# Plain float32 products in place of three split ones, in the query, expert-table and state-space input products of a two-layer backbone

## The chip, the cores and the metric

The kernel runs on one NeuronCore of a Trainium2 chip (trn2). The metric is device microseconds of one execution, the median of several runs. PE is TensorE (PEld its weight load), DVE is VectorE, ACT is ScalarE, POOL is GpSimd, SP is the engine whose queue issues most DMAs.

## The reference, cut to what matters

Two layers, each a token mixer and then a PEER channel mixer, over 512 latent tokens and (in the first layer) 256 context tokens of width 1024, all in float32. Layer 0 mixes with an mLSTM, layer 1 with a Mamba-2 state-space scan (SSD) whose inputs are one product with `w_in` and a five-tap convolution.

```python
def block(xb):                       # PEER, 128 tokens
    q = (xb @ wq).reshape(P_BLOCK, P_HEADS, 2, P_DK // 2)
    s = jnp.einsum('thcd,hcnd->thcn', q, sub_keys)
    s_top, i_top = lax.top_k(s, P_TOPK)          # 16 of 128, twice per head
    ...
    best_s, best_j = lax.top_k(cand_s, P_TOPK)   # 16 of the sums
    idx = jnp.take_along_axis(cand_i, best_j, axis=-1)
    gate = jax.nn.softmax(best_s, axis=-1)
    act = jax.nn.gelu(jnp.einsum('td,thkd->thk', xb, u[idx]))
    return jnp.einsum('thk,thkd->td', gate * act, v[idx])

def prep(h):                         # SSD input
    z, xbc, dt_raw = jnp.split(h @ w_in, [B_DI, B_DI + B_CONV_CH], axis=-1)
    xbc = jax.nn.silu(dw_conv(xbc, conv_w, conv_b))
```

`u` and `v` are tables of 16384 rows, 128 blocks of 128.

## The kernel before, in words

**Split products.** Most weight products are made as three products of the type `float32r`: a weight block `raw` (two slices of 128x512, 512 KB, three buffers) comes from memory, ACT casts it to `whi` (L173), DVE subtracts to get `wlo` (L175), the activations are split alike (`split`, L185 and L186), and `mm3` (L208 to L210) adds hi x hi, hi x lo and lo x hi in PSUM. `ch_steps` uses this with channels as output rows, `tok_steps` with tokens.

**PEER of the latent tokens** (`peer_lat`, one call per layer). `affine_in` transposes and scales the tokens into `pinh`/`pinl`. `peer_scores` makes the queries (4 blocks x 8 slices x 4 outputs x 3 products of 128x512), multiplies them with the keys (L782), and DVE takes the top 16 of each row of 128 (`top16`, L789 to L794). Then a loop over the first 66 blocks of the table `u` (NPRE = 66, `prefix`): 24 products of 128x384 (8 slices x 3), a GELU on ACT (`w`, L977), a store to `aD`. Woven into that loop are `gate_steps`, for 3 of the 4 token tiles (NDENSE = 3): `select` on DVE (L828 to L830 its costly part), then 16 rounds of a one-hot `oh` (L1016), `oa` (L1021), two `og` (L1027) on DVE, and 16 small products on PE per round (L1032), whose result goes to the dense gate table `gD`. The fourth tile, and in layer 0 the context tokens, go another way: `gather_steps` fetches single table rows by indirect DMA on POOL (L860) and DVE multiplies them (L867 for `u`, L878 for `v`). A gather is made to wait for a product (`paced`).

When the gates of all three tiles are written, `dense` runs over all 128 blocks of `v`: `w` is read back from `aD` (blocks below 66) or made by `scores` with `mm3` (the other 62), multiplied with the gates (L1057), split, and multiplied with `v` in 18 products of 128x512.

**The SSD layer.** `ssd_ctx` makes 6 input blocks of the context (256 columns), convolves them, and runs the states; `ssd_lat` makes 12 blocks of the latent tokens (512 columns) and weaves them with the scan (`scan`), in which DVE, ACT and PE take turns and each step reads `bcs` from memory.

**Order.** Each engine runs its instructions in one fixed order, which the scheduler sets from the program's order and its own idea of the times; `PER`, `R_PRE` and other rates say in the program how many gate or gather steps follow a block. SP's queue is in order too.

Of the kernel before, what the change touches and what calls it, by code (L numbers as in the profile page):

```python
# [65 lines left out]
def backbone(ctx: ExitStack, tc: tile.TileContext, A: dict, out: bass.AP):  # L66
# [162 lines left out]

    def ch_block(wt, n, kc, xh, xl, T, eng=None, bank=None):  # L230
# [72 lines left out]
    def make_in(pool, i, cond, js, jc, get, T, xh, xl):  # L303
        sh, sc = mrow(i, cond, js, pool), mrow(i, cond, jc, pool)
        for t in range(T // P):
            x = get(t, pool)
            y = big(pool)
            nc.vector.tensor_tensor(y, x, sc, OP.mult)
            nc.vector.tensor_tensor(y, y, sh, OP.add)
            for half in range(2):  # L310
                o = smb()
                for c in range(4):
                    nc.tensor.transpose(o[:, c * P:(c + 1) * P],
                                        y[:, (half * 4 + c) * P:(half * 4 + c + 1) * P], ident)
                s = (slice(None), slice(half * 4, half * 4 + 4), slice(t * P, (t + 1) * P))
                split(xh[s], xl[s], o.rearrange("p (c t) -> p c t", c=4))
# [43 lines left out]
    def affine_in(pool, i, cond, js, jc, z, T, xh, xl):  # L360


        sh = col(modD[i][cond, js * DM:(js + 1) * DM], pool, "a_sh")
        sc = col(modD[i][cond, jc * DM:(jc + 1) * DM], pool, "a_sc")
        g2, b2 = col(A["ln_g"][i, 0], pool, "a_g"), col(A["ln_b"][i, 0], pool, "a_b")
        nc.vector.tensor_tensor(g2, g2, sc, OP.mult)
        nc.vector.tensor_tensor(b2, b2, sc, OP.mult)
        nc.vector.tensor_tensor(b2, b2, sh, OP.add)
        g, b = row(A["ln_g"][i, 0], pool), row(A["ln_b"][i, 0], pool)
        def mapped(t, half):  # L370
            o = (mxb if half and AFB else smb)()
            to_tok(o, z(t)[:, half * 512:(half + 1) * 512], 4)
            x = pool.tile([P, 4, P], F32, tag="ax", name="ax", bufs=3)
            for c in range(4):
                k = half * 4 + c
                oc = o[:, c * P:(c + 1) * P]
                if c % 2:
                    nc.scalar.activation(x[:, c], oc, AF.Identity, scale=g2[:, k:k + 1], bias=b2[:, k:k + 1])
                else:
                    nc.vector.tensor_scalar(x[:, c], oc, g2[:, k:k + 1], b2[:, k:k + 1], op0=OP.mult, op1=OP.add)  # L380
            return x

        todo = [(t, half) for t in range(T // P) for half in range(2)]
        x = mapped(*todo[0])
        for (t, half), nxt in itertools.zip_longest(todo, todo[1:]):
            y, x = x, mapped(*nxt) if nxt else None
            s = (slice(None), slice(half * 4, half * 4 + 4), slice(t * P, (t + 1) * P))
            split(xh[s], xl[s], y)
# [373 lines left out]
    def peer_scores(pool, i, cond, T, h, inh, inl, side=None):  # L762
# [128 lines left out]
    def peer_lat(i, h, pp, then=lambda: None, close=lambda: None):  # L891
# [7 lines left out]
        with tc.tile_pool(name="pt", bufs=1, reuse_waits="tile") as xp:  # L899
            xh = xp.tile([P, 8, LAT], F32R, name="pinh")  # L900
            xl = xp.tile([P, 8, LAT], F32R, name="pinl")
# [7 lines left out]
            vt, it = peer_scores(xp, i, 0, LAT, h, xh, xl)  # L909
# [25 lines left out]
            with tc.tile_pool(name="pd", bufs=1, reuse_waits="tile") as dp:  # L935
                acc = dense(xp, dp, i, gD, aD, nd, xh, xl)
# [32 lines left out]
    def scores(xp, i, i2, xh, xl, TD, w):  # L969

        so = smb()[:, :TD]
        for half, (uh, ul) in enumerate(wpair(A[f"uT{i}"][i2].rearrange("h p c -> p h c"))):
            for k in range(4):
                s = slice(k * P, (k + 1) * P)
                kk = half * 4 + k
                mm3(so, uh[:, s], ul[:, s], xh[:, kk, :TD], xl[:, kk, :TD], kk == 0, kk == 7)
        nc.scalar.activation(w, so, AF.Gelu_apprx_tanh)  # L977

    def gate_steps(pp, bp, vt, it, gD, t, iot4):
# [117 lines left out]
    def dt_prep(pool, sp, inh, inl, nt):  # L1097
# [5 lines left out]
        with tc.tile_pool(name="sw", bufs=1, reuse_waits="tile") as wq:  # L1103
            w8 = wq.tile([P, 8, 64], F32, name="w8")
            nc.sync.dma_start(w8, A["s_dt"])
            w8h = wq.tile([P, 8, 64], F32R, name="w8h")
            w8l = wq.tile([P, 8, 64], F32R, name="w8l")
            split(w8h, w8l, w8)
            for k in range(8):
                mm3(o[:64, :nt * P], w8h[:, k], w8l[:, k], inh[:, k, :nt * P], inl[:, k, :nt * P], k == 0, k == 7)  # L1110
# [53 lines left out]
    def ssd_in(pool, h):  # L1164
# [3 lines left out]
        inh = pool.tile([P, 8, T], F32R, name="inh")  # L1168
        inl = pool.tile([P, 8, T], F32R, name="inl")

        def steps():
            with tc.tile_pool(name="slr", bufs=1, reuse_waits="tile") as q:
                make_in(q, 1, 0, 0, 1, lambda t, p_: h(t), T, inh, inl)
            dts = dt_prep(pool, pool, inh, inl, nt)
            dtr = next(dts)
            yield inh, inl, dtr, acD
# [10 lines left out]
    def ssd_ctx_in(pool, get, hcp, cinp):  # L1187
# [6 lines left out]
        inh = cinp.tile([P, 8, CTX], F32R, tag="cinh", name="cinh", bufs=1)  # L1194
        inl = hcp.tile([P, 8, CTX], F32R, tag="h_ctx", name="cinl", bufs=1)
        for t, y in enumerate(ys):
            for half in range(2):
# [3 lines left out]
                split(inh[s], inl[s], o.rearrange("p (c t) -> p c t", c=4))  # L1201
        return inh, inl

    def ssd_ctx(inh, inl, SD, lat, rest):
        T, nt = CTX, CTX // P
        with tc.tile_pool(name="sc", bufs=1, reuse_waits="tile") as pool:
            bt = pool.tile([P, nt, 1024], F32, name="bt")
            with tc.tile_pool(name="scv", bufs=1, reuse_waits="tile") as q:
                dts = dt_prep(pool, q, inh, inl, nt)
                for n_, n in enumerate((4, 5, 0, 1, 2, 3)):  # L1210
# [13 lines left out]
                    for c, o in enumerate(ch_block(A["s_in"], 4 + n, 8, inh, inl, T,  # L1224
# [19 lines left out]
    def ssd_lat(h, SD, inh, inl, dtr, acD, dts):  # L1244
# [4 lines left out]
        with ExitStack() as es_:  # L1249
            q = es_.enter_context(tc.tile_pool(name="slq", bufs=1, reuse_waits="tile"))  # L1250

            def channels(n, dst):
                for c, o in enumerate(ch_block(A["s_in"], 4 + n, 8, inh, inl, T)):
# [11 lines left out]
            def project_xz(n):  # L1265
                xt[n] = q.tile([P, nt, 512], F32, tag="xt", name="xt", bufs=2)
                zt[n] = q.tile([P, nt, 512], F32, tag="zt", name="zt", bufs=2)
                for c, o in enumerate(ch_block(A["s_in"], 4 + n, 8, inh, inl, T)):
# [7 lines left out]
                for t, o in enumerate(tok_block(A["s_in"], n, 8, inh, inl, T)):  # L1276
# [234 lines left out]
    cin, rest = peer_lat(0, hl, pp, lambda: ssd_ctx_in(pp, hc, hcpool, cinp), ppx.close)  # L1511
# [3 lines left out]
    with tc.tile_pool(name="sl", bufs=1, reuse_waits="tile") as lp:  # L1515
        lat = ssd_ctx(*cin, SD, ssd_in(lp, hl), rest)
# [79 lines left out]
```

## Time and profile before

| | |
|---|---|
| median of 3 runs | 5928.29 us (5920.93 to 5936.06) |
| profiled execution | 5929.8 us, span 5928.0 us, granted clock 0.937 |
| busy: PE, PEld, DVE | 5272.5 us (89%), 4330.6 us (73%), 4623.1 us (78%) |
| busy: ACT, POOL | 2508.2 us (42%), 1517.6 us (26%) |
| DMA | 1406.96 MB, 236 GB/s over the span |

Busy times are sums over instructions, and a PE matmul's time includes its way through the array, so that a new matmul starts long before the last has ended: what a product costs in a stream is the distance of two starts. The shares are means over stages with different limits; the stages are read one by one.

### The profile page before, as it was taken

The page shows a single profiled execution, that of the slowest core. Times are in us where ns is not written, and L with a number is a line of the kernel's source. Part 1 is how long each engine was busy: PE and PEld are TensorE (multiplying, and loading weights), DVE is VectorE, ACT ScalarE, POOL GpSimd, SP SyncE. Part 2 cuts the span into 40 slices and gives each one's busy share as a digit, 9 for nine tenths or more (in the row PEclk, how much of TensorE's full clock was granted, in tenths as well). Part 3 has the DMA queues.
Part 4 walks back from the last instruction along what each step waited for, and adds up shares of the span by engine and source line. Part 5 has one row for each costly group of instructions (what it writes and reads, how often), then busy time and mean ns, then how long its engine had stood idle before and what let it go on. Part 6 is the DMA issues. An engine that isn't in the chain of part 4 may idle for free.

```text
span 5928.0 us, 76907 instructions
## 1 busy us (share of the span) xinstructions
PE 5272.5 (89%) x25708; PEld 4330.6 (73%) x25708; DVE 4623.1 (78%) x8960; ACT 2508.2 (42%) x5186; POOL 1517.6 (26%) x1284
## 2 busy tenths in 40 slices
PE   6899999999997875998699999788877998799998
PEld 4688777766663444898578899667666898688997
DVE  6743567877676788999888889767776998788888
ACT  4643454322222333344333333477874344333333
POOL 1300001345544445121033444000001011133442
PEclk8999999999998887998799999899888998799999
DMA  6765555898879987566698999433334357798996
GB/s 211 240 191 156 161 164 163 282 333 303 301 248 320 327 313 254 168 198 213 207 340 315 347 336 332 155 97 96 104 110 125 121 180 250 254 339 321 345 339 234
DMA packets 655799, 1406.96 MB, mean 237 GB/s; under 512 B 62760, under 2 KB 237496, under 8 KB 650920
## 3 DMA queue, kind: packets, MB, share of 16 engines
q1 hardware_dynamic: 507944, 865.11, 44.1%
q0 software_dynamic: 147456, 536.94, 25.7%
q8 instruction: 201, 3.29, 0.2%
q14 instruction: 198, 1.62, 0.1%
HBM read 1278.10 MB, written 123.70 MB: 236 GB/s over the span
## 4 chain that ended last, share of the span: by engine, by line
PE 40%; DVE 13%; DMA 13%; issue 6%; ACT 4%; POOL 1%; DVEq 0%; SPq 0%; ACTq 0%; POOLq 0%
PE mm L208 6%; PE mm L209 6%; PE mm L210 6%; PE sm L210 4%; PE sm L208 4%; PE sm L209 4%; DMA g<-in_v_dram,idv 4%; DMA g<-in_u_dram,idx 3%; DVE wlo L175 2%; DMA bcs<-acD 2%; PE mx L1032 2%; PE mx L210 1%; PE mx L208 1%; PE mx L209 1%; DMA raw<-in_v_dram 1%
## 5 line engine op out<-in xcount | busy, mean ns | idle before, releaser
L173 ACT CAST whi<-raw 128x512 fp32r<-128x512 f32 x2032 | 1227.0, 619 | 1815.4 <-PE mm L209 575.7
L175 DVE TENSOR_TENSOR wlo<-raw,whi 128x512 fp32r<-128x512 f32 x1979 | 1348.3, 695 | 499.8 <-ACT whi L173 488.0
L860 POOL DMA_INDIRECT g<-in_u_dram,idx x512 | 623.4, 1218 | 1465.8 <-PE mx L210 418.0
L860 POOL DMA_INDIRECT g<-in_v_dram,idv x512 | 679.3, 1327 | 888.0 <-DVE acc L878 316.8
L878 DVE SCALAR_TENSOR_TENSOR acc<-g,act,acc 128x1024 f32<-128x1024 f32 x508 | 655.7, 1291 | 156.2 <-DMA g<-in_v_dram,idv 153.6
L867 DVE CUSTOM_DVE_ANT_0 g<-g,xb 128x1024 f32<-128x1024 f32 x512 | 622.4, 1220 | 161.8 <-DMA g<-in_u_dram,idx 160.6
L210 PE MATMUL sm<-pinh,wlo 128*128 128x384 f32 x2048 | 693.1, 342 | 14.8 <-DVE wlo L175 14.2
L208 PE MATMUL sm<-pinh,whi 128*128 128x384 f32 x2048 | 697.1, 340 | 4.3 <-ACT w L977 3.0
L209 PE MATMUL sm<-pinl,whi 128*128 128x384 f32 x2048 | 694.2, 339 | 0.0
L209 PE MATMUL mm<-wlo,wh 128*128 128x512 f32 x1024 | 400.6, 394 | 11.1 <-DVE wlo L175 11.0
L210 PEld LDWEIGHTS sm<-pinh,wlo 128*128 128x128 f32 x2048 | 386.0, 189 | 23.2 <-DVE wlo L175 22.5
L210 PE MATMUL mm<-whi,wl 128*128 128x512 f32 x1024 | 393.8, 391 | 3.2 <-DVE wl L186 3.2
L208 PEld LDWEIGHTS sm<-pinh,whi 128*128 128x128 f32 x2048 | 386.5, 189 | 12.6 <-ACT w L977 5.6
L208 PE MATMUL mm<-whi,wh 128*128 128x512 f32 x1024 | 362.5, 396 | 35.0 <-ACT wh L185 31.0
L209 PEld LDWEIGHTS sm<-pinl,whi 128*128 128x128 f32 x2048 | 386.6, 189 | 5.5
L209 PE MATMUL mm<-xcl,whi 128*128 128x256 f32 (+1 forms) x1024 | 349.2, 346 | 8.9 <-DVE xcl L186 8.9
L210 PE MATMUL mm<-xch,wlo 128*128 128x256 f32 (+1 forms) x1024 | 332.0, 349 | 21.6 <-DVE wlo L175 21.4
L208 PE MATMUL mm<-xch,whi 128*128 128x256 f32 (+1 forms) x1024 | 344.3, 349 | 5.1 <-ACT xch L185 4.0
L208 PE MATMUL mm<-inh,whi 128*128 128x512 f32 (+1 forms) x768 | 285.8, 376 | 11.1 <-ACT cva L401 6.9
L1057 DVE TENSOR_TENSOR w<-w,gtb 128x384 f32<-128x384 f32 x256 | 232.5, 912 | 63.8 <-DMA gtb<-gD 28.6
L209 PE MATMUL mm<-inl,whi 128*128 128x512 f32 (+1 forms) x768 | 279.9, 366 | 0.0
L1032 PE MATMUL mx<-og,oa 128*128 128x128 f16 x1536 | 199.2, 297 | 86.3 <-DVE og L1027 86.2
(478 smaller groups left out, 10947.3 us busy)
## 6 DMA issues: line engine op xcount, KB each, us to landing
raw<-in_uT_dram SPq DMA_DIRECT2D x256, 512.0 KB
raw<-in_v_dram SPq DMA_DIRECT2D x256, 512.0 KB
raw<-in_w_qk_dram SPq DMA_DIRECT2D x128, 512.0 KB
raw<-in_ada_w_dram SPq DMA_DIRECT2D x96, 512.0 KB
raw<-in_w_up_dram SPq DMA_DIRECT2D x96, 512.0 KB
gD<-sg SPq DMA_DIRECT2D x48, 1024.0 KB
gtb<-gD SPq DMA_DIRECT2D x32, 1536.0 KB
raw<-in_s_in_dram SPq DMA_DIRECT2D x72, 512.0 KB
```

What stands on the lines that cost most here:

```text
L173: nc.scalar.copy(hi, raw[:, u])
L175: (eng or next(los["eng"])).tensor_tensor(lo, raw[:, u], hi.bitcast(F32), OP.subtract)
L208: nc.tensor.matmul(o, sh, mh, start=start, stop=False)
L209: nc.tensor.matmul(o, sh, ml, start=False, stop=False)
L210: last["pe"] = nc.tensor.matmul(o, sl, mh, start=False, stop=stop)
L860: d = nc.gpsimd.indirect_dma_start(out=g_, out_offset=None, in_=tab, in_offset=bass.IndirectOffsetOnAxis(ap=ix[:, k:k + 1], axis=0))
L867: nc.vector.tensor_tensor_reduce(out=g_, in0=g_, in1=xb, scale=1.0, scalar=0.0, op0=OP.mult, op1=OP.add, accum_out=act[:, k:k + 1])
L878: nc.vector.scalar_tensor_tensor(acc, g_, act[:, k:k + 1], acc, OP.mult, OP.add)
L1032: nc.tensor.matmul(g4[:, k * P:(k + 1) * P], oa[:, f, :, k], og[:, u, :, k], start=u == 0, stop=u == 1)
L1057: nc.vector.tensor_tensor(w, w, gt[0][:, :, j], OP.mult)
```

## The change

Queries of the latent tokens, the 66 blocks of `u` ahead of the dense pass, and all products with the SSD input weights become one plain float32 product each, straight from `raw` (`wraws`), with unsplit activations (`px`, `inx`, `cinx`). The casts and subtractions of those weights and activations go. The dense pass still needs `pinh`/`pinl` for its last 62 blocks, so these are now split from `px` behind the gates. `oh` gets a second buffer. The queries of the context tokens, the mLSTM, both down products and the dense pass stay as they are.

```diff
+    def wraws(wt, n, kc):
+        for k in range(0, kc, 2):
+            raw = raw2(wt[n, k:k + 2].rearrange("k p c -> p k c"))
+            for u in range(2):
+                yield raw[:, u]
+                tick()
...
+    def ch_whole(o, wt, n, kc, x):
...
+        for k, w in enumerate(wraws(wt, n, kc)):
+            for c in range(4):
+                last["pe"] = nc.tensor.matmul(o[c], w[:, c * P:(c + 1) * P], x[:, k, :T], start=k == 0 and not pair,
...
     def ch_block(wt, n, kc, xh, xl, T, eng=None, bank=None):
-        for _ in ch_steps(o, wt, n, kc, xh, xl, eng):
+        for _ in ch_whole(o, wt, n, kc, xh) if xl is None else ch_steps(o, wt, n, kc, xh, xl, eng):
...
@@ affine_in, peer_scores
+            if xl is None:
+                x = xh[:, half * 4:half * 4 + 4, t * P:(t + 1) * P]
...
-                for _ in ch_steps(os_, A["wq"][i], n, 8, inh, inl):
+                for _ in ch_steps(os_, A["wq"][i], n, 8, inh, inl) if cond else ch_whole(os_, A["wq"][i], n, 8, inh):
...
@@ peer_lat
-                scores(xp, i, i2, xh, xl, TD, w)
+                so = smb()[:, :TD]
+                raw = raw2(A[f"uT{i}"][i2].rearrange("h p c -> p h c"))
+                for kk in range(8):
+                    last["pe"] = nc.tensor.matmul(so, raw[:, kk // 4, kk % 4 * P:(kk % 4 + 1) * P], x[:, kk, :TD],
+                                                  start=kk == 0, stop=kk == 7)
+                nc.scalar.activation(w, so, AF.Gelu_apprx_tanh)
...
+                for k in range(8):
+                    split(xh[:, k], xl[:, k], x[:, k, :TD])
...
@@ gate_steps
-                oh = bp.tile([P, 4, P, 4], BF16, tag="oh", name="oh", bufs=1)
+                oh = bp.tile([P, 4, P, 4], BF16, tag="oh", name="oh", bufs=2)
...
@@ ssd_ctx, ssd_lat
-                    for c, o in enumerate(ch_block(A["s_in"], 4 + n, 8, inh, inl, T,
+                    for c, o in enumerate(ch_block(A["s_in"], 4 + n, 8, x_in, None, T,
```

The scheduler also moves instructions. On DVE, at two gate rounds of layer 1's prefix loop, this stands before (`fi`, `g` belong to `select`):

```order
6643 L175 TENSOR_TENSOR wlo_42332<-raw_42312,whi_42330 128x512
6644 L1016 TENSOR_TENSOR oh_40553<-iot4_40246,ct_40406 128x2048
6645 L175 TENSOR_TENSOR wlo_42384<-raw_42380,whi_42382 128x512
6646 L830 TENSOR_REDUCE fi_41478<-g_41455 128x16
6647 L828 TENSOR_TENSOR g_41456<-placek_75,bjb_41477 128x800
6648 L1021 TENSOR_TENSOR oa_40555<-oh_40553,ct_40406 128x1024
6649 L1027 TENSOR_TENSOR og_40557<-oh_40553,cm_40415 128x1024
6650 L1027 TENSOR_TENSOR og_40569<-oh_40553,cm_40415 128x1024
6651 L175 TENSOR_TENSOR wlo_42400<-raw_42380,whi_42398 128x512
6652 L829 TENSOR_TENSOR g_41455<-g_41456 128x800
```

and this now, at a like place of the same loop on DVE:

```order
6299 L864 TENSOR_REDUCE fi_37741<-g_37718 128x16
6300 L862 TENSOR_TENSOR g_38560<-placek_75,bjb_38581 128x800
6301 L1072 TENSOR_TENSOR og_36454<-oh_36450,cm_36232 128x1024
6302 L1072 TENSOR_TENSOR og_36466<-oh_36450,cm_36232 128x1024
6303 L1066 TENSOR_TENSOR oa_36482<-oh_36480,ct_36223 128x1024
6304 L868 CAST idx_37815<-fi_37741 128x128
6305 L863 TENSOR_TENSOR g_38559<-g_38560 128x800
6306 L1061 TENSOR_TENSOR oh_36522<-iot4_36087,ct_36223 128x2048
```

The subtractions are gone from between the rounds; of 173 that stood between layer 1's first transposed token and its first dense step, 11 are left, those of the first `v` blocks.

On PE, at the start of layer 0's queries, this stands before (one row of weights takes 12 products):

```order
8240 L208 MATMUL mm_18783<-pinh_18642,whi_18786 128x512
8241 L209 MATMUL mm_18780<-pinl_18643,whi_18786 128x512
8242 L210 MATMUL mm_18780<-pinh_18642,wlo_18788 128x512
8243 L209 MATMUL mm_18781<-pinl_18643,whi_18786 128x512
8244 L210 MATMUL mm_18781<-pinh_18642,wlo_18788 128x512
```

and this now:

```order
L251 MATMUL mm<-px,raw 128x512 x32
L816 MATMUL mx<-keys,pq 128x128 x4
L251 MATMUL mm<-px,raw 128x512 x2
L816 MATMUL mx<-keys,pq 128x128 x4
L251 MATMUL mm<-px,raw 128x512 x19
```

One block of queries is 32 products instead of 96. Counted over the whole list: in front of layer 1's first gate round PE has 132 plain products of the prefix loop (16.5 blocks; before, 590 split ones, 24.6 blocks), then mostly 10 in front of each of the next 34 rounds (30 and 32 at two), and none before the last 13 of the 48. Layer 0: 112 ahead, mostly 9 to 13 in front of each of the next 40 rounds (33 at one), none before the last 7. On PE nothing differs ahead of layer 0's queries, which start at about 2318 us.

## Rows read from the trace of the kernel before

**Rows 1.** The page's first line.
```profile
span 5928.0 us, 76907 instructions
```
**Rows 2.** Windows: stage, length, busy us of each engine, PE clock, DMA share, GB/s.
```profile
core 0: us, PE busy (x) PEld busy (x) DVE busy (x) ACT busy (x) POOL busy (x), PEclk, DMA share, GB/s
2318.00:2927.00 609.00, 498.57 (x2905) 459.63 (x2905) 552.42 (x1376) 224.27 (x400) 128.09 (x130) 0.88 0.61 190
2990.00:3780.00 790.00, 768.04 (x3763) 676.47 (x3762) 683.35 (x993) 309.88 (x570) 308.70 (x240) 0.99 0.91 325
3780.00:3960.00 180.00, 146.26 (x743) 115.59 (x743) 128.79 (x304) 128.57 (x366) 0.00 (x0) 0.86 0.28 87
3960.00:4470.00 510.00, 421.17 (x1882) 338.04 (x1881) 367.70 (x694) 389.98 (x1146) 0.00 (x0) 0.89 0.34 101
4555.00:5097.00 542.00, 485.87 (x2873) 450.63 (x2873) 481.12 (x1325) 211.07 (x375) 61.21 (x94) 0.91 0.56 178
5010.00:5090.00 80.00, 43.85 (x339) 37.81 (x339) 67.86 (x93) 26.75 (x48) 0.00 (x0) 0.50 0.51 159
```
**Rows 3.** Groups on DVE from 2318 to 2927 us (count, busy, mean ns, idle before).
```profile
L175 DVE TENSOR_TENSOR wlo<-raw,whi 128x512 fp32r<-128x512 f32 x164 | 112.7, 691 | 11.7 <-ACT whi L173 11.7
L878 DVE SCALAR_TENSOR_TENSOR acc<-g,act,acc 128x1024 f32<-128x1024 f32 x50 | 69.5, 1390 | 20.0 <-DMA g<-in_v_dram,idv 19.9
L186 DVE TENSOR_TENSOR pinl<-ax,pinh 128x512 fp32r<-128x512 f32 x8 | 14.4, 1831 | 0.0
```
**Rows 4.** Groups on DVE from 4555 to 5097 us.
```profile
L175 DVE TENSOR_TENSOR wlo<-raw,whi 128x512 fp32r<-128x512 f32 x164 | 111.9, 684 | 37.0 <-ACT whi L173 37.0
L867 DVE CUSTOM_DVE_ANT_0 g<-g,xb 128x1024 f32<-128x1024 f32 x19 | 23.1, 1218 | 0.0
L186 DVE TENSOR_TENSOR pinl<-ax,pinh 128x512 fp32r<-128x512 f32 x3 | 7.5, 2521 | 0.0
```
**Rows 5.** Timeline of DVE at the end of layer 0's gates and layer 1's (start, length).
```profile
2907.04 1.22 DVE L1016 TENSOR_TENSOR oh<-iot,ct 128x2048 bf16<-128x2048 bf16 x1
...
2910.23 1.22 DVE L1016 TENSOR_TENSOR oh<-iot,ct 128x2048 bf16<-128x2048 bf16 x1
...
5097.04 2.39 DVE L1057 TENSOR_TENSOR w<-w,gtb 128x384 f32<-128x384 f32 x3 [14.43 <-DMA gtb<-gD]
```
**Rows 6.** Timeline of PE in layer 1's dense pass: first and last of 12 and of 18.
```profile
5559.77 0.34 PE L208 MATMUL sm<-pinh,whi 128*128 128x384 f32 x1
...
5561.70 0.34 PE L210 MATMUL sm<-pinh,wlo 128*128 128x384 f32 x1
5561.88 0.40 PE L208 MATMUL mm<-whi,wh 128*128 128x512 f32 x1
...
5565.77 0.40 PE L210 MATMUL mx<-whi,wl 128*128 128x512 f32 x1
```
**Rows 7.** Timeline of PEld, weight loads of plain float32 products with 512 columns.
```profile
1406.91 0.19 PEld L558 LDWEIGHTS sm<-qk,kc 128*128 128x128 f32 x1 [0.24 <-issue]
...
1408.63 0.19 PEld L558 LDWEIGHTS sm<-qk,kc 128*128 128x128 f32 x1 [0.24 <-issue]
```
**Rows 8.** Timeline of PE, 256 columns: split products (19 in all), then eight plain ones.
```profile
446.00 0.28 PE L210 MATMUL mm<-xch,wlo 128*128 128x256 f32 x1
...
448.14 0.28 PE L210 MATMUL mm<-xch,wlo 128*128 128x256 f32 x1
448.26 1.89 PE L558 MATMUL sm<-qk 128*128 128x256 f32 x8
```
**Rows 9.** Timeline of PE in layer 1's prefix loop: the products of one gate round.
```profile
4857.95 2.06 PE L1032 MATMUL mx<-og,oa 128*128 128x128 f16 x16
4859.76 0.43 PE L210 MATMUL sm<-pinh,wlo 128*128 128x384 f32 x1
```
**Rows 10.** Groups on DVE from 3960 to 4470 us.
```profile
L175 DVE TENSOR_TENSOR wlo<-raw,whi 128x512 fp32r<-128x512 f32 x96 | 65.2, 685 | 38.7 <-ACT whi L173 34.5 <-PE mm L210 4.2
L1317 DVE TENSOR_TENSOR bcs<-bcs,dt_acs 128x1024 f32<-128x1024 f32 x32 | 39.2, 1225 | 60.3 <-DMA bcs<-acD 60.0
```
**Rows 11.** Chain of work from 3700 to 4560 us: shares by line, two long transfers.
```profile
by line: DMA bcs<-acD 10.9%; PE mm L208 8.5%; PE mm L209 7.9%; PE mm L210 7.9%; DVE cva L403 6.1%; issue 5.0%; ACT wx L1147 4.4%; ACT S L1147 3.1%; DVE wlo L175 2.3%; ACT whi L173 2.2%; DVE bcs L1317 2.0%; PE mx L1343 1.8%; ACT cva L401 1.6
...
3705.80 7.21 DMA raw<-in_uT_dram
3717.57 8.68 DMA raw<-in_s_in_dram
```

More of the change, by code (lines that the diff above doesn't have):

```diff
@@ L186, in split, with parts @@
         nc.vector.tensor_tensor(lo, src, hi.bitcast(F32), OP.subtract)
+    def parts(hi, lo, s, src):
+        if lo is None:
+            nc.scalar.copy(hi[s], src)
+        else:
+            split(hi[s], lo[s], src)
     last = {}
@@ L245, in tok_block @@
         o = [mmb() for _ in range(T // P)]
+        if xl is None:
+            for k, w in enumerate(wraws(wt, n, kc)):
+                for t, x in enumerate(o):
+                    last["pe"] = nc.tensor.matmul(x, xh[:, k, t * P:(t + 1) * P], w, start=k == 0, stop=k == kc - 1)
+            return o
         for _ in tok_steps(o, wt, n, kc, xh, xl):
@@ L372, in mapped @@
             to_tok(o, z(t)[:, half * 512:(half + 1) * 512], 4)
-            x = pool.tile([P, 4, P], F32, tag="ax", name="ax", bufs=3)
+            if xl is None:
+                x = xh[:, half * 4:half * 4 + 4, t * P:(t + 1) * P]
+            else:
+                x = pool.tile([P, 4, P], F32, tag="ax", name="ax", bufs=3)
             for c in range(4):
@@ L387, in affine_in @@
             s = (slice(None), slice(half * 4, half * 4 + 4), slice(t * P, (t + 1) * P))
-            split(xh[s], xl[s], y)
+            if xl is not None:
+                split(xh[s], xl[s], y)
             if half:
@@ L899, in peer_lat @@
         with tc.tile_pool(name="pt", bufs=1, reuse_waits="tile") as xp:
-            xh = xp.tile([P, 8, LAT], F32R, name="pinh")
-            xl = xp.tile([P, 8, LAT], F32R, name="pinl")
+            whole = ExitStack()
+            x = whole.enter_context(tc.tile_pool(name="px", bufs=1, side="right", reuse_waits="tile")).tile(
+                [P, 8, LAT], F32, name="px")
             def prefix(i2):
                 w = xp.tile([P, TD], F32, tag="w", name="w", bufs=3)
-                scores(xp, i, i2, xh, xl, TD, w)
+                so = smb()[:, :TD]
[4 more added lines that the diff above has]
+                nc.scalar.activation(w, so, AF.Gelu_apprx_tanh)
                 nc.sync.dma_start(aD[i2], w)
             back["rate"] = R_WQ
-            vt, it = peer_scores(xp, i, 0, LAT, h, xh, xl)
+            vt, it = peer_scores(xp, i, 0, LAT, h, x, None)
             back["rate"] = 0.0
@@ L935, in peer_lat @@
             with tc.tile_pool(name="pd", bufs=1, reuse_waits="tile") as dp:
+                xh = dp.tile([P, 8, TD], F32R, name="pinh")
+                xl = dp.tile([P, 8, TD], F32R, name="pinl")
+                for k in range(8):
+                    split(xh[:, k], xl[:, k], x[:, k, :TD])
+                whole.close()
                 acc = dense(xp, dp, i, gD, aD, nd, xh, xl)
@@ L1105, in dt_prep @@
             nc.sync.dma_start(w8, A["s_dt"])
-            w8h = wq.tile([P, 8, 64], F32R, name="w8h")
-            w8l = wq.tile([P, 8, 64], F32R, name="w8l")
-            split(w8h, w8l, w8)
             for k in range(8):
-                mm3(o[:64, :nt * P], w8h[:, k], w8l[:, k], inh[:, k, :nt * P], inl[:, k, :nt * P], k == 0, k == 7)
+                nc.tensor.matmul(o[:64, :nt * P], w8[:, k], x_in[:, k, :nt * P], start=k == 0, stop=k == 7)
         a = tp.tile([P, LAT], F32, tag="st", name="st", bufs=3)[:64, :nt * P]
@@ L1193, in ssd_ctx_in @@
                 nc.vector.tensor_tensor(y, y if op == OP.add else get(t), r, op)
-        inh = cinp.tile([P, 8, CTX], F32R, tag="cinh", name="cinh", bufs=1)
-        inl = hcp.tile([P, 8, CTX], F32R, tag="h_ctx", name="cinl", bufs=1)
+        x_in = cinp.tile([P, 8, CTX], F32, tag="cinh", name="cinx", bufs=1)
         for t, y in enumerate(ys):
@@ L1200, in ssd_ctx_in, with ssd_ctx @@
                 s = (slice(None), slice(half * 4, half * 4 + 4), slice(t * P, (t + 1) * P))
-                split(inh[s], inl[s], o.rearrange("p (c t) -> p c t", c=4))
-        return inh, inl
-    def ssd_ctx(inh, inl, SD, lat, rest):
+                parts(x_in, None, s, o.rearrange("p (c t) -> p c t", c=4))
+        return x_in
+    def ssd_ctx(x_in, SD, lat, rest):
         T, nt = CTX, CTX // P
@@ L1252, in channels @@
             def channels(n, dst):
-                for c, o in enumerate(ch_block(A["s_in"], 4 + n, 8, inh, inl, T)):
+                for c, o in enumerate(ch_block(A["s_in"], 4 + n, 8, x_in, None, T)):
                     j = 4 * n + c
@@ L1267, in project_xz @@
                 zt[n] = q.tile([P, nt, 512], F32, tag="zt", name="zt", bufs=2)
-                for c, o in enumerate(ch_block(A["s_in"], 4 + n, 8, inh, inl, T)):
+                for c, o in enumerate(ch_block(A["s_in"], 4 + n, 8, x_in, None, T)):
                     j = 4 * n + c
@@ L1275, in project_xz @@
                     yield
-                for t, o in enumerate(tok_block(A["s_in"], n, 8, inh, inl, T)):
+                for t, o in enumerate(tok_block(A["s_in"], n, 8, x_in, None, T)):
                     silu2(zt[n][:, t], o)
```

29 lines of the change are left out of this document (16 added, 13 removed).

## The prediction

> **What bounds the kernel now.** I read the page's sums (in the table above), then the windows, because the page's shares are means over the whole span [rows 1], but not every stage is PE's. The windows [rows 2] show three kinds. In the dense pass (2990 to 3780 us) PE is busy 768 of 790 us; it keeps its split products, so it stays as it is. In the two stretches from the transposed tokens to the first dense step, 609 us in layer 0 and 542 us in layer 1, DVE is busy 552 and 481 us, more than PE, and DVE's part is not padded: PE's busy time holds each matmul's way through the array. That DVE sets the end shows at the end itself: the last gate rounds follow each other every 3.19 us with DVE full, PE has no table products left, and the dense step waits 14.4 us more for the gates' way through memory [rows 5]. In the SSD stage (3780 to 4470 us) no engine is full: PE 567, DVE 496, ACT 519 of 690 us [rows 2]. There the chain of waits tells more: the three lines of split products hold 24.3% of its 860 us, casts and subtractions 4.5%, transfers of `bcs` 10.9% [rows 11].
>
> **What a product costs.** Split, at full clock: 512 columns (5565.77 - 5561.88) / 17 = 0.229 us, so 0.687 for three; 384 columns (5561.70 - 5559.77) / 11 = 0.1755, 0.527 for three [rows 6]; 256 columns 2.14 / 18 = 0.119, 0.357 for three [rows 8]. Plain float32 products stand in this trace too: with 512 columns their weight loads are (1408.63 - 1406.91) / 4 = 0.43 us apart [rows 7]; with 256 columns eight take 1.89 us, less 0.38 for the last one's way out, over 7: 0.216 [rows 8]. No plain product of 384 columns is there; between 0.216 and 0.43 I take the proportional 0.32. A plain product thus costs 0.61 to 0.63 of three split ones.
>
> The Trainium skill speaks against this: its page FP8 and Floating Point Precision, section TensorE Precision Notes, gives true float32 four passes through the array. By that a 512-column product would take some 0.92 us, more than 0.687, as an estimate from four starts at 0.229. This trace disagrees, with 0.43 us. The trace's 0.43 agrees with the footnote on Perfetto Trace Analysis, section Engine Utilization, which halves the array's rate for a float32 kind.
>
> **Layer 0, transposed tokens to dense, 609 us.** DVE loses 161 of 164 subtractions at 0.691 us: 111 us; its waits for the casts, 11.7 us; the token subtractions, 14.4 us [rows 3]; and the four of `cinl`, near 3 us by the same price. That is 140 us. Eight new subtractions behind the gates (under 0.7 us each, so below 6 us) lie in the 14.4 us for which the gates travel [rows 5] and cost nothing; without that cover, 6 us per layer. What replaces the waits? PE is in order, and its new list puts about 10 plain products in front of each gate round. Such a round takes PE 10 x 0.32 + 1.8 us for its 16 small products (4859.76 - 4857.95 [rows 9]) = 5.0 us; DVE needs 3.19 [rows 5]. Where `select` or gathers fill DVE, this costs nothing. In about 25 of the 48 rounds the list has no `select` between them: PE needs 25 x 5.0 + 7 for a thicker spot = 132 us, DVE 25 x 3.19 + 15 gathers x 1.39 [rows 3] = 101. So 31 us come back as DVE waiting for PE. Gain 109; I take 105, since the gathers' own 20 us of waiting may grow when the rest gets shorter.
>
> **Layer 1, the same stretch, 542 us.** 162 subtractions x 0.684 = 111 us and 37 us of waiting for casts [rows 4]. About 25 rounds without `select` again: PE 25 x 5.0 + 18 for two thicker spots = 143 us, DVE 25 x 3.19 + 20 gathers x 1.22 [rows 4] = 104; 39 us come back. That leaves 109. Raw blocks now stay in their three buffers until the products have read them, and the rounds move 1.25 x (524 + 197) + 524 KB = 1.43 MB in 5.0 us, 285 GB/s, with gathers some 310, near the 325 GB/s of the dense pass [rows 2]; I take off 14 for it, a third of the 39: 95. The token subtractions here are on the way to the first query, 2.5 us each where ACT and PE wait [rows 4]: another 8.
>
> **SSD stage.** On PE the 384 products of the latent tokens save 384 x (0.687 - 0.43) = 99 us and the 192 of the context 192 x (0.357 - 0.216) = 27. Not all is on the chain. It holds 24.3% x 860 = 209 us of split products, of which the input weights have 333 of 461 us by count (576 x 0.119 + 1152 x 0.229, against 88 for the output weights and 40 at the dense tail): 151 us, and 38% of it goes, 57 us. Casts and subtractions hold 4.5%, 39 us; by count three quarters are of input weights: 29 us [rows 11]. Together 86; the paths beside it, first the 60 us of DVE waiting for `bcs` [rows 10], take a little over: 80. Bounds: 29 if only the casts count, 126 if all of PE's saving does.
>
> **Sum.** 105 + 95 + 8 + 80 = 288 us. The profiled execution took 5929.8 us, its span 5928.0, so 1.8 us lie around it; the median of the runs shown is 5928.3, and I make no difference between them. 5930 - 288 = **5642 us**. Nothing ahead of layer 0's queries changes in PE's list, and the dense passes keep their products.
>
> **The rivals.**
>
> *DVE's floor is reached* (13%): the scheduler's list lets PE run far enough ahead, so nothing of the 31 and 39 us comes back, and the SSD stage takes all of PE's saving. 140 + 148 + 8 + 115 = 411: 5519 us. For it speaks that PE's sum in each stretch (62 for queries and keys, 169 for the table, 87 for the rounds, 318 us) stays below DVE's floor near 395; against it, that PE has 16.5 blocks ahead of the first round where it had 24.6.
>
> *Transfers take the place of the subtractions* (22%): three buffers, each held for the transfer and then for eight products. Transfers of `raw` show up to 7.2 us in the chain [rows 11], so a block would come every (7.2 + 2.6) / 3 = 3.3 us in place of 2.6. In 25 rounds with 1.25 blocks that is 22 us per layer, with the queries and the stretch before some 30; the context's input blocks, (8.7 + 1.7) / 3 = 3.5 us against 2.9 before, would lose instead of gain, and `bcs` sits behind such loads in SP's queue: 50 off the SSD stage. 288 - 110 = 178: 5752 us. For it: DMA's share was 0.56 to 0.61 in these stretches and is to move the same bytes in a fifth less time. Against: in the SSD stage it is 0.28 to 0.34 [rows 2].
>
> *The clock falls* (4%, the other side): PE stands idle more, and from 5010 to 5090 us, where it only ran the rounds' small products between waits, the granted clock was 0.50 [rows 2], the lower level of 1.2 GHz. A plain product at that level costs 0.64 us for 384 columns and 0.86 for 512, more than three split ones at 2.4 GHz. If all new products ran so: PE needs 110 for queries, 14 for the keys (64 products at half of 0.43), 338 for the table and 87 for the rounds, 549 us per stretch, layer 0 gains 60, layer 1 loses 7, the SSD stage loses 384 x 0.17 + 192 x 0.075 = 80: 5957 us. It decides below a mean clock of about 0.62, where a plain product costs what three split ones did. Against it: with PE busy 499 of 609 us the clock was 0.88, and it rises where products stand in rows.
>
> *Four passes after all* (2%), as an operand kind unlike that of [rows 7] might have: 0.92 us for 512 columns and 0.70 for 384. PE would need 118 + 7 + 370 + 87 = 582 us per stretch, minus 27 and plus 40 us against 609 and 542, and lose 384 x 0.23 + 192 x 0.12 = 111 in the SSD stage: 6054 us. That is what the page FP8 and Floating Point Precision of the Trainium skill would make of the change.
>
> The forecast itself has 58% and alone spans 5580 to 5705; 1% is left for no change. A measurement of this kernel can tell about 0.3%, some 18 us, from none. So faster 0.93, same 0.02, slower 0.05. The range takes in the floor and the transfers' case: **5515 to 5752 us**.
>
> **What would show it.** In the profile after: no `wlo` from `uT`, `wq` or `s_in`; plain products of 512, 384 and 256 columns starting 0.43, 0.32 and 0.216 us apart in rows; DVE busy near 430 and 365 us in the two stretches, now near 505 and 440 us long; gate rounds between table products 4.5 to 5.5 us apart, with `og` waiting for the PSUM tile of the round before; first dense step still 14 us behind the last round; the dense passes within 1% of 790 and 768 us. The forecast is wrong if DVE's waits name `raw` by way of PE (transfers), if the clock in the two stretches is under 0.65, or if the SSD stage keeps its 690 us.

## The result, and the profile after

The changed kernel takes 6011.35 us (median of 4 runs, 6000.28 to 6021.33) beside 5932.18 for the kernel before on the same chip: ratio 1.0125, 95% interval 1.01 to 1.015. It is 1.25% slower; the forecast was 5642 us. The page's first lines after, for [rows 1]:

```profile
span 6013.5 us, 71451 instructions
...
PE 5495.7 (91%) x23804; PEld 4056.9 (67%) x23804; DVE 4329.7 (72%) x8474; ACT 2242.8 (37%) x4712; POOL 1514.1 (25%) x1284
```

DVE lost 293 us of work, as meant (4623.1 before), and PE, which was to lose some, gained 223 (5272.5 before). The windows after, to be read against [rows 2]; columns as there:

```profile
2318.00:2924.00 606.00, 567.30 (x2237) 355.37 (x2237) 456.59 (x1210) 128.56 (x232) 98.90 (x132) 0.96 0.61 196
2990.00:3743.00 753.00, 733.63 (x3535) 645.13 (x3534) 657.19 (x944) 288.44 (x528) 311.66 (x239) 1.00 0.92 332
3743.00:3960.00 217.00, 200.47 (x725) 130.07 (x725) 112.66 (x284) 116.75 (x343) 0.00 (x0) 0.92 0.32 103
3960.00:4500.00 540.00, 461.16 (x1504) 268.77 (x1502) 319.90 (x608) 341.17 (x1055) 0.00 (x0) 0.88 0.32 94
4587.00:5177.00 590.00, 559.24 (x2217) 348.88 (x2215) 382.31 (x1170) 121.60 (x221) 54.01 (x98) 0.96 0.52 164
```

In both stretches from the transposed tokens to the first dense step, PE and DVE have changed places: PE 567 of 606 and 559 of 590 us, DVE 457 and 382. DVE's sums are near the forecast (430 and 365); the lengths are not (505 and 440). The granted clock is 0.96 in both, higher than before.

Why PE is full stands in the records of the new products (a record is one row that the profiler keeps; the listing puts neighbours of one kind together, with their number behind the x). PE's timeline, in rows of plain products: the context's state-space inputs (256 columns), the latent ones (512), and layer 1's prefix loop (384), where `sm<-px,raw` are the plain table products and `mx<-og,oa` the 16 small ones of a gate round.

```profile
3757.22 15.38 PE L251 MATMUL mm<-cinx,raw 128*128 128x256 f32 x70
...
4260.70 7.89 PE L251 MATMUL mm<-inx,raw 128*128 128x512 f32 x18
...
4957.14 2.05 PE L1077 MATMUL mx<-og,oa 128*128 128x128 f16 x16
4959.01 6.63 PE L943 MATMUL sm<-px,raw 128*128 128x384 f32 x20
4965.48 2.04 PE L1077 MATMUL mx<-og,oa 128*128 128x128 f16 x16
4967.34 6.63 PE L943 MATMUL sm<-px,raw 128*128 128x384 f32 x20
```

Twenty records stand between the two rounds shown. The list of instructions has mostly 10 products there. All records of that line, then those of the queries and the state-space inputs, by line:

```profile
L943 PE MATMUL sm<-px,raw x2112: 483/486/590, 2452.5 to 5127.2; 128*128 128x384 f32 x192
...
L251 PEld LDWEIGHTS mm<-px,raw x512: 186/190/337, 2322.1 to 4706.4; 128*128 128x128 f32 x171
L251 PE MATMUL mm<-px,raw x512: 592/592/1221, 2322.1 to 4706.8; 128*128 128x512 f32 x171
...
L251 PE MATMUL mm<-inx,raw x512: 592/592/1223, 3868.5 to 4277.5; 128*128 128x512 f32 x171
...
L251 PE MATMUL mm<-cinx,raw x384: 379/379/794, 3743.7 to 3863.9; 128*128 128x256 f32 x192
```

The program issues 2 layers x 66 blocks x 8 = 1056 table products; there are 2112 records. The queries are 2 x 128 = 256 products and 512 records, the context's inputs 192 and 384. A split product has one record: `sm<-pinh,whi` before stands 2048 times for 2 x 128 blocks x 8. So **a plain float32 product is two matmul records here**, and its price is two spacings: (6.63 - 0.49) / 19 = 0.323 us apart with 384 columns, 0.646 a product; with 512, (7.89 - 0.59) / 17 = 0.429, 0.859 a product; with 256, (15.38 - 0.38) / 69 = 0.217, 0.435 a product (each time the row's length less the last record's own, over the steps between records).

Against three split products (0.527, 0.687 and 0.357 us, from [rows 6, 8]) that is 1.22 to 1.25 times as much; the forecast had 0.61 to 0.63. The two-record form was in the trace of before as well. By line:

```profile
L558 PE MATMUL sm<-qk,kc x64: 591/592/697, 1405.9 to 1812.8; 128*128 128x512 f32 x64
```

The loop at L558 issues 32 of these (4 heads, 2 row blocks of `kc`, 4 pieces each). The four spacings of [rows 7] were two products, and the eight records of [rows 8] four.

DVE's view of the same: `og` waits for the PSUM tile of the round before, about 5 us in each round, and the rounds are 8.34 us apart (forecast 5.0).

```profile
4958.28 0.69 DVE L1072 TENSOR_TENSOR og<-oh,cm 128x1024 f16<-128x1024 bf16 x1 [4.06 <-PE mx L1077]
...
4966.62 0.69 DVE L1072 TENSOR_TENSOR og<-oh,cm 128x1024 f16<-128x1024 bf16 x1 [4.96 <-PE mx L1077]
...
4974.96 0.69 DVE L1072 TENSOR_TENSOR og<-oh,cm 128x1024 f16<-128x1024 bf16 x1 [4.97 <-PE mx L1077]
```

The chart of waits (total, times, longest) over layer 1's stretch, over layer 0's, and over the state-space stage:

```profile
DVE og L1072 <- PE mx L1077: 88.4, 41, 6.1
...
DVE og L1072 <- PE mx L1077: 90.9, 44, 5.0
...
DVE bcs L1357 <- DMA bcs<-acD: 110.2, 32, 6.0
```

For `og` 39 and 31 us had been forecast to come back. Before, `og` had no such wait in layer 1's stretch and 1.0 us of it in layer 0's; there PE's small products waited for `og`, in layer 1's stretch:

```profile
PE mx L1032 <- DVE og L1027: 34.6, 23, 4.8
```

All kernels of this study by stage, us, each from its own trace. The bounds are starts: the first transposition of the latent state ahead of layer 0's queries, the first dense step of layer 0, the first product of the context's state-space inputs, the first mapped token of layer 1, layer 1's first dense step, and the end of the span.

| kernel | ahead | layer 0 to dense | dense 0 | state space | layer 1 to dense | dense 1, end | span |
|---|---|---|---|---|---|---|---|
| before | 2298.3 | 629.3 | 820.0 | 791.0 | 558.4 | 831.0 | 5928.0 |
| after | 2302.1 | 622.4 | 819.2 | 836.9 | 597.1 | 835.8 | 6013.5 |
| e1_half | 2303.7 | 503.2 | 821.9 | 726.0 | 427.9 | 836.7 | 5619.4 |
| e2_peer_only | 2298.4 | 621.3 | 818.9 | 791.1 | 600.4 | 834.3 | 5964.4 |
| e3_ssd_only | 2295.8 | 626.2 | 816.3 | 832.2 | 556.9 | 834.1 | 5961.5 |
| e4_oh2 | 2295.8 | 626.9 | 826.1 | 789.2 | 548.0 | 833.9 | 5919.9 |
| e5_query | 2294.0 | 620.0 | 814.7 | 795.6 | 557.0 | 832.4 | 5913.7 |
| e6_prefix | 2288.3 | 627.4 | 812.1 | 800.2 | 589.4 | 835.1 | 5952.6 |
| e7_mix | 2289.7 | 618.9 | 810.9 | 794.7 | 575.2 | 829.3 | 5918.7 |
| e8_ctx | 2292.7 | 630.6 | 820.8 | 783.0 | 558.2 | 828.3 | 5913.6 |
| e9_mixed | 2290.3 | 613.8 | 820.0 | 783.9 | 548.6 | 827.6 | 5884.2 |
| e10_mixed2 | 2283.0 | 616.2 | 816.6 | 779.1 | 548.3 | 833.2 | 5876.4 |

Of the 85.5 us that the changed kernel lost in these profiles, 45.9 are in the state-space stage and 38.7 in layer 1's stretch; layer 0's gives 6.9 back. The stages whose code is the same in all kernels (ahead, dense) differ by up to 21 us from profile to profile, so a stage's difference under 10 us is not read alone. The two stretches repeat better where their code is the same: layer 1's takes 556.9 to 558.4 us in the three kernels that have it as before (before, e3, e8) and 548.0 to 548.6 in the three that add only a second `oh` buffer (e4, e9, e10); layer 0's takes 626.2 to 630.6 in before, e3 and e8.

### The profile page after: what moved, and what is told of

The parts are those of the page before. It is cut to its first block, busy times and chain, and to the rows that moved or that the text cites. A ratio compares the mean times of both kernels' runs of the same rounds, so it can differ in the third digit from the quotient of the medians.

```text
span 6013.5 us, 71451 instructions
## 1 busy us (share of the span) xinstructions
PE 5495.7 (91%) x23804; PEld 4056.9 (67%) x23804; DVE 4329.7 (72%) x8474; ACT 2242.8 (37%) x4712; POOL 1514.1 (25%) x1284
## 4 chain that ended last, share of the span: by engine, by line
PE 40%; DMA 15%; DVE 12%; issue 7%; ACT 3%; POOL 1%; SPq 0%; DVEq 0%; POOLq 0%; ACTq 0%
PE sm L943 8%; PE mm L251 6%; DMA g<-in_v_dram,idv 5%; DMA g<-in_u_dram,idx 4%; PE mm L224 3%; PE mm L223 3%; PE mm L225 3%; DMA bcs<-acD 3%; PE sm L225 2%; PE sm L223 2%; PE sm L224 2%; PE mx L1077 2%; DVE g L901 1%; DVE wlo L175 1%; PE mx L225 1%
## 5 line engine op out<-in xcount | busy, mean ns | idle before, releaser
L173 ACT CAST whi<-raw 128x512 fp32r<-128x512 f32 x1560 | 936.2, 619 | 1316.7 <-PE mm L224 413.7
L175 DVE TENSOR_TENSOR wlo<-raw,whi 128x512 fp32r<-128x512 f32 x1507 | 1026.1, 698 | 384.3 <-ACT whi L173 376.0
L943 PE MATMUL sm<-px,raw 128*128 128x384 f32 x2112 | 697.3, 486 | 3.3 <-ACT w L945 3.3
L943 PEld LDWEIGHTS sm<-px,raw 128*128 128x128 f32 x2112 | 395.7, 191 | 261.4 <-ACT w L945 3.9
L225 PE MATMUL sm<-pinh,wlo 128*128 128x384 f32 x992 | 335.8, 339 | 0.0
L223 PE MATMUL sm<-pinh,whi 128*128 128x384 f32 x992 | 335.8, 338 | 0.0
L224 PE MATMUL sm<-pinl,whi 128*128 128x384 f32 x992 | 335.4, 338 | 0.0
L193 ACT CAST wh<-w 128x384 fp32r<-128x384 f32 x256 | 131.7, 514 | 332.1 <-DVE w L1102 235.4
L223 PEld LDWEIGHTS mm<-whi,wh 128*128 128x128 f32 x1024 | 193.3, 189 | 75.1 <-ACT wh L193 31.9
L251 PE MATMUL mm<-inx,raw 128*128 128x512 f32 x512 | 236.6, 614 | 6.1 <-ACT cva L435 3.4
```

The costliest lines, as they stand in the source:

```text
L173: nc.scalar.copy(hi, raw[:, u])
L175: (eng or next(los["eng"])).tensor_tensor(lo, raw[:, u], hi.bitcast(F32), OP.subtract)
L223: nc.tensor.matmul(o, sh, mh, start=start, stop=False)
L224: nc.tensor.matmul(o, sh, ml, start=False, stop=False)
L225: last["pe"] = nc.tensor.matmul(o, sl, mh, start=False, stop=stop)
L251: last["pe"] = nc.tensor.matmul(o[c], w[:, c * P:(c + 1) * P], x[:, k, :T], start=k == 0 and not pair, stop=k == kc - 1 and not (pair and ...
```

## The experiments

**e1_half: every second slice left out.** Of the plain products only the even slices k are issued, so the sums lack half their terms; all loads, buffers and casts stay. The order of the rest does not: the scheduler puts 30 blocks ahead of layer 1's first gate round, where the changed kernel has 16.5, and none ahead of the last 28 of the 48 rounds (in the changed kernel's trace, of the last 12). The edit, in the three places:

```diff
-                for kk in range(8):
+                for kk in range(0, 8, 2):
...
-            for c in range(4):
+            for c in range(4 if k % 2 == 0 else 0):
...
-                for t, x in enumerate(o):
+                for t, x in enumerate(o if k % 2 == 0 else []):
```

> The changed kernel with every second slice of the contraction left out of the plain products (queries, table blocks, state-space inputs); all of the weights are still loaded into the same three buffers and each buffer is still held until a product has read it. Price theory (a plain product is two matmuls on the chip, so 0.86 us for 512 columns and 0.64 for 384): TensorE's load falls to what the prediction had reckoned with, so the two stretches before the dense passes should take about 505 and 440 us, the state-space stage about 700 us, the whole 5600 to 5700 us. Buffer theory (held buffers and transfers are the limit): the bytes are the same, so 5950 to 6010 us. Order theory (the scheduler's new order and the second one-hot buffer cost the time): 5950 to 6010 us as well.

Measured: 5613.0 us, ratio 0.9453 (0.9433 to 0.9472). With half of the products, PE spends on them what the forecast had reckoned for all of them, and the kernel comes out 29 us under the forecast. Its records, by line, are 1056 for 528 products, so the halving did not change what one product leaves:

```profile
L943 PE MATMUL sm<-px,raw x1056: 483/486/1009, 2435.9 to 4665.4; 128*128 128x384 f32 x176
```

The windows of the two stretches show PE off the end and DVE back on it, with all raw blocks still transferred through the same three buffers, at a higher rate than in the changed kernel:

```profile
2318.00:2806.00 488.00, 369.32 (x1581) 233.92 (x1581) 448.88 (x1213) 127.19 (x232) 121.07 (x133) 0.82 0.75 242
4361.00:4782.00 421.00, 346.67 (x1561) 224.21 (x1560) 375.68 (x1170) 121.17 (x221) 59.22 (x98) 0.86 0.72 229
```

With the products' time on PE, 398 us went away. That excludes the transfers as the cause of the loss in the two stretches. It does not hold the order fixed, and a buffer is held for a shorter time too when its products are halved. Against the order in layer 1's stretch speaks PE's own sum: at the spacings above the changed kernel needs 128 x 0.859 + 528 x 0.646 + 48 x 1.8 = 537 us there, without the keys, so no order brings that stretch near the 440 us of the forecast; before, the same sum was 128 x 0.687 + 528 x 0.527 + 48 x 1.8 = 453.

**e2_peer_only and e3_ssd_only: one part each.** e2 has the plain queries and table blocks (and the second `oh` buffer) with the state-space inputs split as before; e3 has the plain state-space inputs alone.

> Only the queries and the first 66 table blocks plain (and the second one-hot buffer); the state-space inputs split as before. Price theory: layer 1's stretch as in the changed kernel (about 590 us instead of 542), layer 0's level, state-space stage as before: 5960 to 5980 us. If the loss were all in the state-space stage: 5930 us.

> Only the state-space inputs plain. Price theory: TensorE gains 192 x 0.07 us for the context and 384 x 0.17 us for the latent tokens, 79 us, of which the changed kernel showed 46 us from the first context product to layer 1's first transposed token (837 us against 791): 5965 to 5985 us, and the two stretches before the dense passes as before. If the loss sat in the table stretches alone: 5930 us or less.

Measured: e2 5958.88 us, ratio 1.0046 (1.003 to 1.0062); e3 5956.13, ratio 1.0034 (1.0019 to 1.005). e2 lies 1 us below its range and e3 9 us below. Each part loses in its own stage: e2's layer 1 stretch is 42 us longer, e3's state-space stage 41 us, and the other stages stay within 10 us. Neither is a gain spoilt by the other.

**e4_oh2: the second buffer alone.** The kernel before with one number changed:

```diff
-                oh = bp.tile([P, 4, P, 4], BF16, tag="oh", name="oh", bufs=1)
+                oh = bp.tile([P, 4, P, 4], BF16, tag="oh", name="oh", bufs=2)
```

> The kernel before with only the second buffer for the one-hot tile. Price theory: no change, 5930 us within 0.3%. Order theory: a part of the 80 us, 5960 us or more.

Measured: 5916.73 us, ratio 0.9981 (0.9968 to 0.9993). The table puts 10 us of it into layer 1's stretch. The changed kernel has this buffer too; if it gains as much there, its products cost that much more than the net difference shows.

**e5_query, e6_prefix, e7_mix: which products of the stretches.** In e5 only the queries are plain, in e6 only the 66 table blocks, both with two `oh` buffers; in e7 the queries and the odd blocks, with one buffer, since the parts and the whole tokens are both kept:

```diff
+                if i2 % 2:
+                    so = smb()[:, :TD]
...
+                                                      start=kk == 0, stop=kk == 7)
+                    nc.scalar.activation(w, so, AF.Gelu_apprx_tanh)
+                else:
+                    scores(xp, i, i2, xh, xl, TD, w)
```

> Only the 128 query products per layer are plain; the table blocks and the state-space inputs are split as before; oh has its second buffer. Theory P (a plain product of 512 columns costs two records of 0.43 us, 0.86, against 0.687 split): PE gets 128 x 0.17 = 22 us more per layer and DVE loses 32 subtractions and the token subtractions, some 36 us. Layer 0's stretch, where DVE sets the end, gains 0 to 20 us, layer 1's loses 5 to 20, the second buffer gives its 11: 5915 to 5945 us. Rival (a product costs 0.43 and the loss came from somewhere else): PE saves 33 us per layer and the stretches with it, 5860 us or less.

> Only the 66 table blocks per layer are plain (528 products of 384 columns); queries and state-space inputs split; oh has its second buffer. Theory P: 0.64 us a product against 0.527, so PE gets 528 x 0.115 = 61 us more per layer, DVE loses 132 subtractions (91 us). Layer 0's stretch, bounded by DVE before and by PE after, stays within 15 us of before; layer 1's loses 20 to 35 us: 5930 to 5955 us. With e5 the two parts should add up to e2's 36 us in layer 1. Rival (buffers and transfers of raw blocks make the rounds wait, whatever PE does): the loss of layer 1 is here alone and e5 has none.

> Queries plain, the odd ones of the 66 blocks plain, the even ones split, state-space inputs split; oh has one buffer as before. Theory P: half of the 61 us of PE and half of the 91 us of DVE, so that the two engines are nearer to each other: PE near 535 and DVE near 505 us in layer 0's stretch. Layer 0 gains 10 to 35 us, layer 1 loses 5 to 20: 5900 to 5935 us. Rival (raw blocks in few buffers): both stretches lose about half of what e2 loses.

Measured, in this order: 5924.45 us, ratio 0.9982 (0.9969 to 0.9995); 5957.91, ratio 1.0047 (1.0022 to 1.0073); 5926.2, ratio 0.9993 (0.998 to 1.0005). In layer 1, against e4, which has the same `oh` buffers, the queries cost 557.0 - 548.0 = 9 us and the blocks 589.4 - 548.0 = 41; together 50, and e2, with both, has 52. PE's own price would be 128 x (0.859 - 0.687) = 22 and 528 x (0.646 - 0.527) = 63. So the loss has the order of the price in both, less what DVE's saved subtractions give back. Against the kernel before e5's stretch is level, and by that alone it would fit the rival of e6's expectation; the second buffer hides its 9 us. Layer 0's stretch gains 9 us in e5, in the middle of what was expected, and 10 in e7, at the low end; e6 came out 3 us above its range. In e7 layer 1 loses 17 us, of which the queries are 9: half the blocks cost 8, under half of 41. PE and DVE are then nearer to each other, here in layer 0:

```profile
2318.00:2908.00 590.00, 538.07 (x2497) 393.10 (x2497) 493.30 (x1272) 165.83 (x303) 99.65 (x126) 0.94 0.63 195
```

**e8_ctx: the context's inputs alone.** As e3, with the latent inputs split again (`x_in, inl` in `ssd_lat` as before).

> Only the state-space stage's inputs of the context are plain (192 products of 256 columns and the first step sizes); the latent ones, the queries and the table blocks are split. Theory P: 0.43 us a product against 0.357, so 14 us more of PE, and 48 subtractions and as many casts less on DVE and ACT. Between -10 and +10 us, 5918 to 5938; e3's 28 us then come from the latent products, 384 x 0.175 = 67 us of PE. Rival (one of the changed buffers or loads of the context costs the 28 us): 5945 us or more.

Measured: 5915.4 us, ratio 0.9965 (0.9951 to 0.9979). It gains, and comes out 3 us below its range. The context's 192 products run from 3747.6 to 3887.1 us before and from 3744.1 to 3867.3 here. The stretch from 3765 us, and the next 30 us, before and in e8 (PE, PEld, DVE, ACT, POOL, clock, DMA):

```profile
3765.00:3790.00 25.00, 21.92 (x157) 20.13 (x155) 24.05 (x50) 13.90 (x25) 0.00 (x0) 0.93 0.41 129
3790.00:3820.00 30.00, 20.11 (x113) 17.22 (x114) 25.35 (x61) 21.36 (x40) 0.00 (x0) 0.78 0.29 92
```
```profile
3765.00:3790.00 25.00, 25.00 (x118) 20.07 (x117) 22.09 (x60) 12.08 (x24) 0.00 (x0) 1.00 0.43 132
3790.00:3820.00 30.00, 28.68 (x139) 23.41 (x138) 22.88 (x49) 15.65 (x29) 0.00 (x0) 1.00 0.43 135
```

Before, DVE is busy 24 of 25 us and PE waits, at a granted clock that goes down to 0.78; with plain products PE is full at 1.00, and the dearer product comes out ahead. Half of the 16 us that the context's part gains is lost again behind it: the whole stage is 8 us shorter. Over all traces the context's part takes 134.7 to 139.6 us with split products (6 kernels) and 119.2 to 123.2 with plain ones (5, without e1).

The latent tokens are the other case: from the last context product to the first mapped token of layer 1 the kernel before takes 4538.6 - 3887.1 = 651 us, the changed one 4580.6 - 3863.9 = 717. The price says 384 x (0.859 - 0.687) = 66, and the difference is 65. That close a fit is partly chance: in the nine kernels with split latent inputs this part takes 651 to 665 us, and before is the shortest. e3 and e8, which differ in the latent inputs alone, have 713.0 and 659.8, 53 us apart.

**e9_mixed and e10_mixed2: plain where PE has room.** Both have e8's plain context, layer 1 and the latent inputs split, and two `oh` buffers in layer 1. In layer 0, e9 has e7's mix with one buffer; e10 has plain queries, split blocks and two buffers.

> Plain products only where PE had room: the context's state-space inputs, and in layer 0 the queries and every second table block (oh with one buffer there); layer 1 and the latent inputs split, oh with two buffers in layer 1. Theory P with the stages measured so far: layer 0's first dense step 19 us earlier as in the mix, layer 1's stretch 10 us shorter as with the second buffer alone, the state-space stage 8 to 16 us shorter as with the context alone: 37 to 45 us in all, 5880 to 5900 us. Rival (the gains are one and the same slack, found three times): 20 us or less, 5908 us or more.

> As e9, but layer 0's table blocks all split and oh with two buffers in both layers: plain are the context's inputs and layer 0's queries. Theory P: layer 0's first dense step 14 us earlier as in the run with plain queries, layer 1's stretch 10 us and the state-space stage 8 to 16 us shorter: 32 to 40 us, 5886 to 5904 us. Rival as for e9.

Measured: e9 5888.46 us, ratio 0.9926 (0.9909 to 0.9943); e10 5884.92, ratio 0.9928 (0.991 to 0.9946). Both beat the kernel before and the changed one, and are not told apart from each other; e10 lies 1 us below its range. By the table layer 1's stretch gives 10 us, the state-space stage 7 to 12, layer 0's stretch 13 to 16. Another 8 to 15 us lie ahead of layer 0's stretch in these two profiles, in code that no edit touches; no run tells why. The three gains of the table add up to 32 us in e9 and 35 in e10, so they are not one slack found three times, but the 37 to 45 us expected of e9 were reached only with the unexplained part.

## Why the prediction was wrong

**The step that failed is "What a product costs": 0.43, 0.32 and 0.216 us for a plain product, "0.61 to 0.63 of three split ones".** The spacings were read rightly and hold in the trace after to the second digit. What was wrong is what they are spacings of: records were taken for products, without counting the records of L558 against its loop. A product is two records, 0.859, 0.646 and 0.435 us, and every term with a product in it had the wrong sign on PE's side. "Eight take 1.89 us" were four.

**The rule that the prediction set aside came near the measurement.** The Trainium skill's page FP8 and Floating Point Precision, section TensorE Precision Notes, gives true float32 four passes; the trace now shows 0.859 us against 0.229 for one split product, 3.75 times, and 3.7 for 384 and 256 columns. The prediction wrote "this trace disagrees, with 0.43 us", which was the miscount. The footnote in the Trainium skill's page Perfetto Trace Analysis, section Engine Utilization, which halves the rate and was cited beside it, comes near one record (0.429 against 0.229 us), not one product.

**Layer 0, 105 us forecast, 7 came.** DVE's busy time fell from 552 us [rows 2] to 457 (near 430 was forecast), and this step's subtractions are gone. With ten products at 0.646 a round is 6.5 + 1.9 = 8.3 us in place of 5.0, and PE, busy 567 of 606 us, set the pace of the rounds until its table products ran out. The end itself came as forecast: the last `og`, the splits of the held tokens behind the gates, and the dense step 14.5 us after that `og`:

```profile
2910.03 0.69 DVE L1072 TENSOR_TENSOR og<-oh,cm 128x1024 f16<-128x1024 bf16 x1 [0.25 <-PE mx L1077]
2917.88 3.84 DVE L194 TENSOR_TENSOR pinl<-px,pinh 128x384 fp32r<-128x384 f32 x8 [7.15 <-DMA gD<-sg]
```

**Layer 1, 95 and 8 us forecast, 39 lost.** The same cause with less slack: the stretch before was shorter (542 us, with DVE busy 481 [rows 2], against 609 and 552), while PE's price is the same 22 + 63 us, which here outweighs what the subtractions give back.

**State space, 80 us forecast, 46 lost.** The latent part lost 65 us (53 between e3 and e8) where it was to give most of the gain; the context's 19 us (139.5 before, 120.2 after) came in spite of its price, because there DVE was in the way, which the stage's sums [rows 2] do not show and a window of 25 us does. DVE's waits for `bcs` [rows 10] grew, from 60.0 to 110.2 us. They are 110.4 us in e3, 61.0 in e8 and 75.8 in e1_half, which has the same loads and half the products: they grow with the latent products' time, not with the bytes. In the chain of work from 3743 to 4580 us the transfers of `bcs` now hold 18.0% of 837, 151 us, where they held 10.9% of 860, 94 us [rows 11]:

```profile
by line: PE mm L251 23.8%; DMA bcs<-acD 18.0%; PE mm L274 5.6%; DVE bcs L1357 4.0%; DVE cva L437 3.3%; issue 2.1%; PE sm L1197 2.0%; ACT bcs L1365 1.9%; DVE m L1367 1.7%; ACT m L1365 1.6%; PE sm L1152 1.6%; ACT wx L1189 1.6%; DVE bcs L1359 
```

So part of what the products cost here may reach the end by way of `bcs`. In SP's queue, which issues the loads of `raw` and of `bcs` in order, the loads of `raw` waited 210 us for subtractions before and now wait 184 and 74 us for the plain products of L251 and L274. The rival of the transfers had put 50 us on `bcs` behind held buffers. How the products' time makes these waits longer, no run shows, and in this stage held buffers stay possible as the way.

**The rest of the sum came close in total, less so in its parts.** e1_half gives PE the product time that the forecast assumed, by leaving out half of the products, and comes to 5613 us beside 5642; its stages gain 126, 131 and 65 us where 105, 103 and 80 were forecast. The two stretches, above their forecast, and the state-space stage, below it, partly cancel. Nor did the 31 and 39 us of DVE waiting for PE appear there (`og` waits for PE 0 and 6.3 us): e1_half has another order, with more table blocks ahead of the rounds. PE's waits that end with a transfer of `raw` come to 15.3 us in layer 0's stretch and 8.4 in layer 1's, so the rival of the transfers was small in the stretches.

**The rivals.** "Four passes after all" had 2%, and it is the one that came: 27 us gained, 40 and 111 lost, 6054 us, beside 7, 39 and 46, and 6011. That it ends only 43 us off is partly luck: its state-space term is 65 us too high, because of 0.92 us where 0.859 was measured and because it counted the context as a loss, and its gain in layer 0 is 20 us too high. The clock did not fall: 0.96 in both stretches.

## What to carry to other kernels

Before a duration is taken from a row as the price of an operation, count the row's records against the instructions that the program issues there; a plain float32 product here is two records and costs a quarter more than three products of split operands. Replacing work on two engines by dearer work on a third pays only where the first two set the end, and that is read in windows of a few tens of us: the same edit gave 19 us in the context's part of the stage and took 65 in the latent one, of which 53 are shown by two kernels that differ in nothing else. A change that is right in one stage and wrong in the next is best made per stage, as e9 and e10 do.

## What had not been expected of the hardware

A plain product leaves two matmul records and two weight loads (x512 each for 256 products of the queries), each with the shape of the whole product, so nothing in these rows says that one is a half.

The prices above are those of rows at the full clock. At the start of the context's products before, split ones of 256 columns start 0.21 us apart, which is 0.64 for three (at a granted clock of 0.72 from 3747 to 3756 us); a few us later they are 0.12 apart. The plain ones after begin the same way, at 0.79 from 3743 to 3753 us: their first records are 0.43 us apart, which is 0.86 a product, against 0.217 and 0.435 later. So the plain product is the dearer one there too:

```profile
3748.18 0.41 PE L210 MATMUL mm<-cinh,wlo 128*128 128x256 f32 x1
3748.39 0.41 PE L208 MATMUL mm<-cinh,whi 128*128 128x256 f32 x1
```
```profile
3743.72 5.82 PE L251 MATMUL mm<-cinx,raw 128*128 128x256 f32 x18
```
